# Slot places and norm rows moved between the gate and up products of a mixture-of-experts stage

## The chip, the core and the metric

The kernel runs on one core of a Trainium2 chip. The metric is the device time of one execution in microseconds (us): the median of several runs. The core has five engines that work side by side and wait for each other by semaphores: TensorE (PE; PEld is its weight load), VectorE (DVE), ScalarE (ACT), GpSimd (POOL) and SyncE (SP, which issues the DMAs here).

## What is computed

The reference is a decoder trunk of two layers over 512 tokens of width 1024, in float32. Each layer has a token mixer (attention in layer 0, a pooling mixer in layer 1), a layer norm, a mixture of 32 SwiGLU experts with two experts chosen per token, and another layer norm. The change touches the mixture alone:

```python
def run_block(args):
    xb, e = args
    h = jax.nn.silu(xb @ w_gate[e]) * (xb @ w_up[e])
    return h @ w_down[e]
...
out = jnp.zeros((N, D), x.dtype).at[tok_pad].add(y * w_pad[:, None].astype(y.dtype))
...
h = layer_norm(DEEPNORM_ALPHA * h + ffn, ln_g[i, 1], ln_b[i, 1])
```

Gate and up weights are 1024 x 512 per expert, down weights 512 x 1024: 6 MB per expert in float32, 384 MB for both layers.

## The kernel before

Function `moe` handles a layer's mixture. Experts are taken in 16 pairs; each expert of a pair has 64 slots (`CAP`), so a pair fills the 128 columns or rows of a tile. The loop over `q` (8 passes) handles two pairs, an even one `2q` and an odd one `2q + 1`. For a pair the work is:

- **Gather.** `G` is a matrix of zeros and ones that says which token sits in which slot, built for two pairs at once by VectorE (lines 583 and 584, eight instructions). TensorE multiplies the tokens with it (line 919) in four rounds of 16 products of 128 x 256 for each of two chunks; each round fills one PSUM bank, which ScalarE and VectorE empty into `xT`, scaled by the first norm's gain (lines 903, 905). In this kernel the rounds take the banks `ga`, `tp`, `ga`, `tp` in turn.
- **Gate and up.** `gate_up` makes 16 products for the gate (`psg`) and 16 for the up projection (`psu`), line 960, each two instructions in the trace, since a float32 product takes two; the two experts of a pair use the two halves of the array's columns. ScalarE makes silu of the gate (`sg`), VectorE multiplies (`h`, line 969).
- **Flip and down.** `flip` transposes `h` on TensorE into bank `tp` (line 974), ScalarE copies it to `hT`, and `down` makes 16 products `y` (line 985; 32 instructions). ScalarE and VectorE scale `y` by the slot's weight `ws` into `yy` as a high and a low part (lines 994, 995).
- **Places.** `places` transposes `G` of a pair into bank `ga` (line 934), which ScalarE copies to `Sm`; four products with the routing weights `wd` (`pw`, line 938) give, through `pwc`, the slot weights `ws`. Both pairs' places are made in the even pair's turn, just ahead of its down product.
- **Spread.** `spread_all` brings `yy` of the two pairs of the pass before back to the tokens through `Sm` (lines 1161, 1162, eight banks of four products, in the two `sc` banks); VectorE adds each bank to the residual `R` (line 1164). It stands in the even pair's turn, around the flip.

Two pieces occur once a layer. In pass 0, `whole` sums the tokens into `R` on GpSimd (line 1135), and after the odd pair's gather `residue` makes four norm rows (`norm_row`, line 384, four products or eight instructions each, with the gain or shift broadcast) which VectorE applies to `R` (lines 1143, 1145). In the last pass, `norm_rows` makes four rows of the second norm in bank `ga`, each copied by ScalarE into `gb` (line 390), between the spreads and the places.

`wd` of all pairs comes at the start of the stage out of a chain on VectorE and ScalarE that runs beside the first gate product (lines 1037 to 1048 and 257). GpSimd's `whole` runs beside it. After the last pair, where the routing needs it, `seek` and `down_spread` handle one extra item in the same way, and `norm_all` ends the layer.

TensorE's order in this stage is the order in which the code is written (`manual_schedule` for PE); the other engines' orders are made by a scheduler. Weight loads are issued by SyncE in one queue (`fill`, `take`), each into one of 21 buffers of 1 MB (`unit`) as soon as the work that read the buffer before is done.

Of the kernel before, what the change touches and what calls it, by code (L numbers as in the profile page):

```python
# [41 lines left out]
WARM2 = 2  # L42
REGION = {mybir.EngineType.PE, mybir.EngineType.DVE, mybir.EngineType.Activation, mybir.EngineType.Pool}
# [21 lines left out]
def tile_trunk(ctx, tc, x, w_qkv, w_o, p_in, p_grp, p_scale, p_out,  # L65
# [826 lines left out]
    def moe(l, rt_in, name1, after):  # L892
        with ExitStack() as es:
# [13 lines left out]
            def gather(slots, cc, xT, pairs):  # L907
# [16 lines left out]
                def ga_tile(k0):  # L924
                    return p1.tile([P, 2, 2 * P], F32, name="ga", tag=("ga", "tp")[k0 // 2 % 2])
# [3 lines left out]
            def places(G, i, wd, Sm, ws):  # L929

                ga = p1.tile([P, NT, P], F32, name="ga", tag="ga")
                gi = G[:, :, i * P:(i + 1) * P]
                for j, t in enumerate(tiles):
                    PE.transpose(ga[:, t], gi[:, j].bitcast(F32), ident)
                ACT.activation(Sm[:, :].rearrange("p (t q) -> p t q", t=NT), ga, AF.Copy)
                pw = p1.tile([P, 4], F32, name="pw", tag="tp")
                for t in range(NT):
                    PE.matmul(pw, gi[:, t], wd[:, t], start=t == 0, stop=t == NT - 1)
                pc = mo.tile([P, 4], F32, name="pwc", tag="pwc")
                V.tensor_copy(pc, pw)  # L940
                for e in range(2):
                    es_ = slice(e * CAP, (e + 1) * CAP)
                    V.tensor_tensor(ws[es_], pc[es_, e:e + 1], pc[es_, 2 + e:3 + e], op=OP.add)
# [138 lines left out]
            def place(G, p):  # L1082
                Sm = mo.tile([P, S], F32R, name="Sm", tag="Sm", bufs=3)
                ws = mo.tile([P, 1], F32, name="ws", tag="ws", bufs=3)
                places(G, p % 2, wd[:, :, p], Sm, ws)
                plc[p] = Sm, ws

            def seek(xT1, Sm1):
# [22 lines left out]
                places(G1, 0, wx, Sm1, ws1)  # L1111
# [15 lines left out]
            def bank():  # L1127
                return p1.tile([P, 512], F32, name="row", tag="ga")

# [7 lines left out]
            def residue(q, tag):  # L1137

                ps = norm_row(l, 0, q, p2.tile([P, 512], F32, name="row", tag=tag))
                for t in tiles:  # L1140
                    r = tok(R, t)[:, q % 2 * 512:(q % 2 + 1) * 512]
                    if q < 2:
                        V.scalar_tensor_tensor(r, r, ALPHA, ps, op0=OP.mult, op1=OP.mult)
                    else:
                        V.scalar_tensor_tensor(r, ps, ALPHA, r, op0=OP.mult, op1=OP.add)
# [6 lines left out]
            def spread_all(c, ys):  # L1152

                for t in range(NT):
                    spread_sum([(yr, Sm) for yr, Sm in ys], t, c)
# [10 lines left out]
            def gate_of(p):  # L1166
                h = h_tile()
                gate_up(xT[:, :, (p % 2) * P:(p % 2 + 1) * P],
                        [[take(nm, l, p, e) for e in range(2)] for nm in "gu"], h)
                done(8)  # L1170
                return h
# [10 lines left out]
            for q in range(NPAIR // 2):  # L1182
# [3 lines left out]
                h = gate_of(p)  # L1186
# [6 lines left out]
                if prev:  # L1193
                    spread_all(0, prev)
                hT = hT_tile()
# [3 lines left out]
                if final:  # L1199
                    gb, rows_ = norm_rows(l, 1, bank)  # L1200
                    do(rows_)
                place(G, p)
                place(G, p + 1)
# [4 lines left out]
                h = gate_of(p)  # L1208
# [19 lines left out]
                else:  # L1228
                    fill(CAPW)
                    xT, (G, rounds) = gather2(p + 1)  # L1230
                    rows_ = [lambda i=i: residue(i, "sc") for i in (0, 2, 1, 3)] if q == 0 else []
# [3 lines left out]
                    do(rounds[2:4] + rows_)  # L1235
# [110 lines left out]
```

## Time and profile before

| | |
|---|---|
| median of 3 runs | 1574.7 us (1573.53 to 1575.3) |
| the profiled execution | 1572.45 us |
| its span | 1570.7 us |
| TensorE busy | 1459.1 us (93%), 7477 instructions |
| VectorE busy | 629.3 us (40%) |
| ScalarE busy | 364.3 us (23%) |
| GpSimd busy | 102.0 us (6%) |
| read from HBM | 446.74 MB, 286 GB/s over the span |

The profile comes from one execution; the difference between its time and its span is 1.75 us. Mixture 0 runs from about 311 us, mixture 1 from about 1026 us of the span, each with eight passes. A row of a timeline gives the start, the duration up to the end of the last instruction of the row, the engine and line, what is written and read, how often, and in brackets the engine's idle time before it with what ended it. Rows that follow each other overlap by the latency of an instruction, so lengths are best taken from start to start. A row of windows gives a stretch and its length, then the busy time of PE, PEld, DVE, ACT and POOL with the number of instructions, TensorE's granted clock (1.00 is 2.4 GHz, 0.50 is 1.2 GHz; between them it is the mean over the stretch), the share of time that the DMA engines were busy, and their rate in GB/s. The stretches below begin and end where rows of TensorE's timeline begin: a repeating pass from odd gate product to odd gate product; the first pair of each layer from its up product to the next gate product; pass 0 from the end of the odd pair's up product to the next gate product; the last pass from its first norm row to the odd pair's gate product.

### The profile page before, as it was taken

What the parts mean: (1) busy time and instruction counts of PE and PEld (TensorE: products, weight loads), DVE (VectorE), ACT (ScalarE), POOL (GpSimd) and SP (SyncE); (2) the same over time, 40 slices, a digit from 0 to 9 for tenths busy, and PEclk for the clock granted to TensorE, in tenths of its full rate; (3) what the DMA queues carried; (4) which work ended last, traced back from release to release, by engine and by line L of the source; (5) the groups of instructions that cost most, each with busy time, mean ns of one, the idle gap of its engine ahead of it and who ended that gap; (6) DMA issues with size and microseconds to landing.
All of it is one profiled execution on the core that took longest, in us unless ns stands there. A gap on an engine that the chain in (4) does not pass through costs nothing. (4 is left out here: it accounts for less than half of the span.)

```text
span 1570.7 us, 18886 instructions
## 1 busy us (share of the span) xinstructions
PE 1459.1 (93%) x7477; PEld 838.0 (53%) x7477; DVE 629.3 (40%) x1447; ACT 364.3 (23%) x736; POOL 102.0 (6%) x66
## 2 busy tenths in 40 slices
PE   8999999998999999999998589998999999999993
PEld 6766777734544454445542467844455445444541
DVE  4366466643331322323233986653322213313216
ACT  4355464511111111111110323521111011111110
POOL 0000000320000000000004610230000000000001
PEclk9999999999999999999899899999999999999987
DMA  7111422677999999999865116567999999999921
GB/s 250 46 54 49 166 112 77 268 305 300 414 402 403 414 407 403 408 406 415 353 268 210 33 54 241 210 266 295 412 408 412 397 410 411 398 407 414 406 105 55
DMA packets 85571, 450.20 MB, mean 287 GB/s; under 512 B 10648, under 2 KB 20448, under 8 KB 36320
## 3 DMA queue, kind: packets, MB, share of 16 engines
q1 hardware_dynamic: 85472, 448.86, 71.6%
q8 instruction: 64, 1.05, 0.3%
q14 instruction: 35, 0.29, 0.1%
HBM read 446.74 MB, written 2.10 MB: 286 GB/s over the span
## 5 line engine op out<-in xcount | busy, mean ns | idle before, releaser
L960 PE MATMUL psg<-w_g,xT 128*64 128x512 f32 x1024 | 225.2, 592 | 0.2 <-ACT xT L903 0.2
L960 PE MATMUL psu<-w_u,xT 128*64 128x512 f32 x1024 | 225.1, 592 | 0.0
L985 PE MATMUL y<-w_d,hT 128*64 128x512 f32 x960 | 224.2, 622 | 0.0
L995 DVE SCALAR_TENSOR_TENSOR yy<-y,ws,yy 128x512 fp32r<-128x512 f32 x66 | 48.6, 737 | 395.1 <-ACT yy L994 394.4
L960 PEld LDWEIGHTS psu<-w_u,xT 128*64 128x64 f32 x1024 | 73.3, 137 | 146.4 <-issue 142.7
L960 PEld LDWEIGHTS psg<-w_g,xT 128*64 128x64 f32 x1024 | 73.1, 137 | 145.9 <-issue 141.4
L985 PEld LDWEIGHTS y<-w_d,hT 128*64 128x64 f32 x960 | 69.0, 143 | 131.1 <-issue 129.2
L919 PEld LDWEIGHTS ga<-G,xs 128*128 128x128 f32 x960 | 114.0, 188 | 12.2 <-issue 12.2
L919 PE MATMUL ga<-G,xs 128*128 128x256 f32 x960 | 119.6, 282 | 0.0
L967 ACT ACTIVATE sg<-psg 128x512 f32<-128x512 f32 x33 | 19.7, 597 | 423.5 <-PE psg L960 423.5
L1161 PE MATMUL sc<-yy,Sm 128*128 128x512 f32 x240 | 102.0, 425 | 6.7 <-DVE r L1164 6.1
L1164 DVE TENSOR_TENSOR r<-r,sc 128x512 f32<-128x512 f32 x128 | 85.9, 684 | 36.1 <-PE sc L1162 36.1
L969 DVE TENSOR_TENSOR h<-sg,psu 128x512 f32<-128x512 f32 x33 | 35.6, 1078 | 161.2 <-PE psu L960 150.4
L1162 PE MATMUL sc<-yy,Sm 128*128 128x512 f32 x240 | 94.8, 395 | 0.0
L288 PE MATMUL acc<-pc,xTh 128*128 128x512 f32 x192 | 77.6, 404 | 2.6 <-ACT pc L256 2.3
L289 PE MATMUL acc<-pc,xTh 128*128 128x512 f32 x192 | 77.1, 402 | 0.8 <-DVE pc L257 0.8
L290 PE MATMUL acc<-pc,xTl 128*128 128x512 f32 x192 | 77.6, 404 | 0.0
L905 DVE TENSOR_SCALAR xT<-ga,gcol 128x256 f32<-128x256 f32 (+1 forms) x60 | 32.1, 535 | 107.7 <-ACT xT L903 107.7
L903 ACT ACTIVATE xT<-ga,gcol 128x256 f32<-128x256 f32 (+1 forms) x60 | 33.4, 557 | 151.9 <-PE ga L919 151.9
L1161 PEld LDWEIGHTS sc<-yy,Sm 128*128 128x128 f32 x240 | 45.1, 188 | 41.9 <-DVE r L1164 22.1
L994 ACT ACTIVATE yy<-y,ws 128x512 fp32r<-128x512 f32 x66 | 45.2, 684 | 79.5 <-PE y L1013 36.2
L975 ACT ACTIVATE hT<-tp 128x512 f32<-128x512 f32 x33 | 19.7, 598 | 182.3 <-PE tp L974 182.3
(303 smaller groups left out, 1923.7 us busy)
## 6 DMA issues: line engine op xcount, KB each, us to landing
w_g<-in_moe_w_gate_dram SPq DMA_DIRECT2D x128, 1024.0 KB
w_u<-in_moe_w_up_dram SPq DMA_DIRECT2D x128, 1024.0 KB
w_d<-in_moe_w_down_dram SPq DMA_DIRECT2D x128, 1024.0 KB
w_a<-in_attn_w_qkv_dram SPq DMA_DIRECT2D x16, 512.0 KB
x<-in_x_dram SPq DMA_DIRECT2D x8, 512.0 KB
w_v<-in_attn_w_qkv_dram SPq DMA_DIRECT2D x4, 1024.0 KB
w_wo<-in_attn_w_o_dram SPq DMA_DIRECT2D x4, 1024.0 KB
wx<-in_moe_w_gate_dram SPq DMA_DIRECT2D x4, 1024.0 KB
```

Of the source, the lines that this page charges most:

```text
L288: PE.matmul(acc, xhl(0, k), wh, start=start and j == 0, stop=False)
L289: PE.matmul(acc, xhl(0, k), wl, start=False, stop=False)
L290: PE.matmul(acc, xhl(1, k), wh, start=False, stop=stop and j == len(order) - 1)
L919: PE.matmul(ga[:, k - k0], half_of(xs[j], i).bitcast(F32R)[:, k], g, start=j + i == 0, stop=j + i == NT)
L960: PE.matmul(ps[es_], xT[:, k, es_], ws2[e][k // 4][:, k % 4], start=k == 0, stop=k == KD - 1)
L969: V.tensor_tensor(h[:, :, :].rearrange("s k q -> s q k"), r(sg), r(gu[1]), op=OP.mult)
L985: PE.matmul(y[es_, c], hT[:, k, es_], wd(e, k, c), start=k == 0, stop=k == 3)
L994: ACT.activation(yr[:, c], y[:, c], AF.Copy, scale=wslot)
L995: V.scalar_tensor_tensor(yr[:, 2 + c], y[:, c], wslot, yy[:, c], op0=OP.mult, op1=OP.subtract)
L1161: PE.matmul(ps, sm, yr[:, c], start=i == 0, stop=False)
L1162: PE.matmul(ps, sm, yr[:, 2 + c], start=False, stop=i == len(ys) - 1)
L1164: V.tensor_tensor(r, r, ps, op=OP.add)
```

## The change

- `places` is cut into `flip_places` (the transposes of one pair into bank `ga` and the copy to `Sm`) and `slot_weights` (the eight `pw` products of two pairs, one copy, four additions). `place` hands out two lists. `gate_of` has a new argument `between`, and runs what is in it between the pair's last gate product and its first up product. The even pair gets its own transposes and both pairs' `pw` products there, the odd pair its own transposes.
- The norm rows go to the same gaps, two rows (eight products, 16 instructions) in a gap, in the `sc` banks: `residue` in the gaps of pairs 1 and 2, `norm_rows` in those of pairs 14 and 15.
- The gather's second and third rounds use the `sc` banks instead of `tp` and `ga`; the fourth uses `ga`.
- In pass 0, which has no spreads, 9 products of 128 x 256 in bfloat16 that nobody reads stand ahead of the transposes of `h`, and 5 behind them (`WARM5`, `WARM6`).

The arithmetic stays as it was. Blank lines are left out.

```diff
--- before.py
+++ after.py
@@ -40,6 +40,8 @@
 WARM3 = 24
 WARM4 = 10
 WARM2 = 2
+WARM5 = 9
+WARM6 = 5
 REGION = {mybir.EngineType.PE, mybir.EngineType.DVE, mybir.EngineType.Activation, mybir.EngineType.Pool}
 FILL2 = 3
@@ -922,25 +924,36 @@
                         factor(xT[:, k, 0:n], ga[:, k - k0, 0:n], k, (ACT, V)[k % 2])
                 def ga_tile(k0):
-                    return p1.tile([P, 2, 2 * P], F32, name="ga", tag=("ga", "tp")[k0 // 2 % 2])
+                    if k0 in (2, 4):
+                        return p2.tile([P, 2, 2 * P], F32, name="ga", tag="sc")
+                    return p1.tile([P, 2, 2 * P], F32, name="ga", tag="ga")
                 return G, [lambda k0=k0: round(k0, ga_tile(k0)) for k0 in range(0, KD, 2)]
-            def places(G, i, wd, Sm, ws):
-                ga = p1.tile([P, NT, P], F32, name="ga", tag="ga")
-                gi = G[:, :, i * P:(i + 1) * P]
+            def flip_places(G, i, Sm, ga):
                 for j, t in enumerate(tiles):
-                    PE.transpose(ga[:, t], gi[:, j].bitcast(F32), ident)
+                    PE.transpose(ga[:, t], G[:, j, i * P:(i + 1) * P].bitcast(F32), ident)
                 ACT.activation(Sm[:, :].rearrange("p (t q) -> p t q", t=NT), ga, AF.Copy)
-                pw = p1.tile([P, 4], F32, name="pw", tag="tp")
-                for t in range(NT):
-                    PE.matmul(pw, gi[:, t], wd[:, t], start=t == 0, stop=t == NT - 1)
-                pc = mo.tile([P, 4], F32, name="pwc", tag="pwc")
-                V.tensor_copy(pc, pw)
-                for e in range(2):
-                    es_ = slice(e * CAP, (e + 1) * CAP)
-                    V.tensor_tensor(ws[es_], pc[es_, e:e + 1], pc[es_, 2 + e:3 + e], op=OP.add)
+            def slot_weights(G, todo, pw):
+                for i, (wd, ws) in enumerate(todo):
+                    for t in range(NT):
+                        PE.matmul(pw[:, 4 * i:4 * i + 4], G[:, t, i * P:(i + 1) * P], wd[:, t],
+                                  start=t == 0, stop=t == NT - 1)
+                n = len(todo)
+                pc = mo.tile([P, 8], F32, name="pwc", tag="pwc")
+                V.tensor_copy(pc[:, 0:4 * n], pw[:, 0:4 * n])
+                for i, (wd, ws) in enumerate(todo):
+                    for e in range(2):
+                        es_ = slice(e * CAP, (e + 1) * CAP)
+                        V.tensor_tensor(ws[es_], pc[es_, 4 * i + e:4 * i + e + 1],
+                                        pc[es_, 4 * i + 2 + e:4 * i + 3 + e], op=OP.add)
+            def places(G, wd, Sm, ws):
+                flip_places(G, 0, Sm, p1.tile([P, NT, P], F32, name="ga", tag="ga"))
+                slot_weights(G, [(wd, ws)], p1.tile([P, 8], F32, name="pw", tag="tp"))
             def run(todo):
                 if todo:
@@ -1080,10 +1093,15 @@
             plc = {}
             def place(G, p):
-                Sm = mo.tile([P, S], F32R, name="Sm", tag="Sm", bufs=3)
-                ws = mo.tile([P, 1], F32, name="ws", tag="ws", bufs=3)
-                places(G, p % 2, wd[:, :, p], Sm, ws)
-                plc[p] = Sm, ws
+                for i in range(2):
+                    Sm = mo.tile([P, S], F32R, name="Sm", tag="Sm", bufs=3)
+                    ws = mo.tile([P, 1], F32, name="ws", tag="ws", bufs=4)
+                    plc[p + i] = Sm, ws
+                flips = [lambda i=i: flip_places(G, i, plc[p + i][0], p1.tile([P, NT, P], F32, name="ga", tag="ga"))
+                         for i in range(2)]
+                return [flips[0], lambda: slot_weights(G, [(wd[:, :, p + i], plc[p + i][1]) for i in range(2)],
+                                                       p1.tile([P, 8], F32, name="pw", tag="tp"))], flips[1:]
             def seek(xT1, Sm1):
@@ -1108,7 +1126,7 @@
                 V.tensor_scalar(rem, rem, 0.0, None, op0=OP.max)
                 G1, rounds = gather(sl, code, xT1, 1)
                 do(rounds)
-                places(G1, 0, wx, Sm1, ws1)
+                places(G1, wx, Sm1, ws1)
             def fetch(w, pr, u2):
                 wv = w[l].rearrange("e (p k) n -> e p (k n)", p=P)
@@ -1124,9 +1142,6 @@
                         nc.sync.dma_start(u2[c][e], wv[bass.ds(pr[e], 1), :, :, c * 512:(c + 1) * 512]
                                           .rearrange("a p k n -> (a p) k n"))
-            def bank():
-                return p1.tile([P, 512], F32, name="row", tag="ga")
             def whole(c):
                 for j, t in enumerate(tiles):
@@ -1134,9 +1149,9 @@
                     hi, lo = [half_of(xs[j], i)[:, :, c * 64:(c + 1) * 64] for i in range(2)]
                     nc.gpsimd.tensor_tensor(rq, hi, lo, op=OP.add)
-            def residue(q, tag):
-                ps = norm_row(l, 0, q, p2.tile([P, 512], F32, name="row", tag=tag))
+            def residue(q):
+                ps = norm_row(l, 0, q, p2.tile([P, 512], F32, name="row", tag="sc"))
                 for t in tiles:
                     r = tok(R, t)[:, q % 2 * 512:(q % 2 + 1) * 512]
                     if q < 2:
@@ -1163,10 +1178,12 @@
                 r = tok(R, t)[:, c * 512:(c + 1) * 512]
                 V.tensor_tensor(r, r, ps, op=OP.add)
-            def gate_of(p):
+            def gate_of(p, between=()):
                 h = h_tile()
                 gate_up(xT[:, :, (p % 2) * P:(p % 2 + 1) * P],
-                        [[take(nm, l, p, e) for e in range(2)] for nm in "gu"], h)
+                        [[take(nm, l, p, e) for e in range(2)] for nm in "gu"], h,
+                        todo=[lambda: do(between)], at=(KD - 1,))
                 done(8)
                 return h
@@ -1183,7 +1200,13 @@
                 p, final = 2 * q, q == NPAIR // 2 - 1
                 fill(CAPW)
-                h = gate_of(p)
+                if final:
+                    gb, rows_ = norm_rows(l, 1, lambda: p2.tile([P, 512], F32, name="row", tag="sc"))
+                else:
+                    rows_ = [lambda i=i: residue(i) for i in (0, 2, 1, 3)]
+                placed, placed2 = place(G, p)
+                h = gate_of(p, placed if q == 0 else (placed + rows_[0:2] if final else
+                                                      placed + rows_[2:4] if q == 1 else placed))
                 if q == 0:
                     R = two("r")
                     whole(0)
@@ -1192,20 +1215,20 @@
                 fill(CAPW)
                 if prev:
                     spread_all(0, prev)
+                else:
+                    wps = p2.tile([P, 512], F32, name="wps", tag="sc")
+                    warm(wps, WARM5)
                 hT = hT_tile()
                 flip(h, hT)
                 if prev:
                     spread_all(1, prev)
-                if final:
-                    gb, rows_ = norm_rows(l, 1, bank)
-                    do(rows_)
-                place(G, p)
-                place(G, p + 1)
+                else:
+                    warm(wps, WARM6)
                 prev = [down_of(p, hT, wdn)]
                 p += 1
                 fill(5 if final else CAPW)
-                h = gate_of(p)
+                h = gate_of(p, placed2 + (rows_[2:4] if final else rows_[0:2] if q == 0 else []))
                 wdn = [take("d", l, p, i) for i in range(2)]
                 Sm, ws = plc[p]
                 if final:
@@ -1228,11 +1251,10 @@
                 else:
                     fill(CAPW)
                     xT, (G, rounds) = gather2(p + 1)
-                    rows_ = [lambda i=i: residue(i, "sc") for i in (0, 2, 1, 3)] if q == 0 else []
                     do(rounds[0:2])
                     hT = hT_tile()
                     flip(h, hT)
-                    do(rounds[2:4] + rows_)
+                    do(rounds[2:4])
                     prev.append(down_of(p, hT, wdn))
```

TensorE, even pair of pass 1 (`sc` is a spread, `ga` the transposes of `G`, `pw` the weight products, `row` norm rows, `y` a down product). Before, at the end of the spreads:

```order
L1162 MATMUL sc<-yy,Sm 128x512
L934 MATMUL ga<-cf,G 128x128 x4
L938 MATMUL pw<-wd,G 128x4 x4
L934 MATMUL ga<-cf,G 128x128 x4
L938 MATMUL pw<-wd,G 128x4 x4
L985 MATMUL y<-w_d_2_0_0_3224,hT 64x512
```

Now, between the pair's gate and up products (line numbers are the changed kernel's):

```order
L973 MATMUL psg<-w_g_2_1_1_3244,xT 64x512
L936 MATMUL ga<-cf,G 128x128 x4
L943 MATMUL pw<-wd,G 128x4 x8
L386 MATMUL row<-vec,cf 128x128 x8
L973 MATMUL psu<-w_u_2_0_0_3246,xT 64x512
```

The places left the stretch between spread and down product for the one between gate and up; in pass 1 two norm rows follow them.

TensorE, odd pair of pass 0, from the up product to the down product. Before:

```order
L960 MATMUL psu<-w_u_1_0_1_3095,xT 64x512
L960 MATMUL psu<-w_u_1_1_1_3097,xT 64x512
L919 MATMUL ga<-G,xs 128x256 x32
L974 MATMUL tp<-cf,h 128x128 x4
L919 MATMUL ga<-G,xs 128x256 x32
L384 MATMUL row<-vec,cf 128x128 x16
L985 MATMUL y<-w_d_1_0_0_3099,hT 64x512
```

Now, ahead of the up product:

```order
L973 MATMUL psg<-w_g_1_0_1_3036,xT 64x512
L973 MATMUL psg<-w_g_1_1_1_3038,xT 64x512
L936 MATMUL ga<-cf,G 128x128 x4
L386 MATMUL row<-vec,cf 128x128 x8
L973 MATMUL psu<-w_u_1_0_0_3040,xT 64x512
```

The 16 products of the norm rows no longer stand between the gather and the down product; eight of them follow the transposes of `G` here, the other eight stand in the next pair, above.

VectorE, odd pair of pass 0 (`G` is rebuilt for the next pass, `r` are the residue's steps). Before:

```order
L583 TENSOR_SCALAR G<-cf,cc 128x256
L943 TENSOR_TENSOR ws<-pwc 64x1 x2
L584 SCALAR_TENSOR_TENSOR G<-cf,cc,G 128x256
L583 TENSOR_SCALAR G<-cf,cc 128x256 x2
L584 SCALAR_TENSOR_TENSOR G<-cf,cc,G 128x256 x2
L583 TENSOR_SCALAR G<-cf,cc 128x256
L584 SCALAR_TENSOR_TENSOR G<-cf,cc,G 128x256
L1024 TENSOR_SCALAR cc<-code 128x8
L995 SCALAR_TENSOR_TENSOR yy<-y,ws,yy 128x512
L969 TENSOR_TENSOR h<-sg,psu 128x128x4
```

Now, between the first pair's `h` and the second's:

```order
L585 TENSOR_SCALAR G<-cf,cc 128x256 x2
L586 SCALAR_TENSOR_TENSOR G<-cf,cc,G 128x256 x2
L1158 SCALAR_TENSOR_TENSOR r_3109<-r_3109,row 128x512 x2
L1158 SCALAR_TENSOR_TENSOR r_3108<-r_3108,row 128x512 x2
L1160 SCALAR_TENSOR_TENSOR r_3109<-row,r_3109 128x512 x2
L1160 SCALAR_TENSOR_TENSOR r_3108<-row,r_3108 128x512 x2
L585 TENSOR_SCALAR G<-cf,cc 128x256 x2
L586 SCALAR_TENSOR_TENSOR G<-cf,cc,G 128x256
L1008 SCALAR_TENSOR_TENSOR yy<-y,ws,yy 128x512
L586 SCALAR_TENSOR_TENSOR G<-cf,cc,G 128x256
L1037 TENSOR_SCALAR cc<-code 128x8
L982 TENSOR_TENSOR h<-sg,psu 128x128x4
```

The residue's first eight steps stand inside the rebuilding of `G`, which now waits for the odd pair's transposes.

## Rows read from the trace of the kernel before

**Rows 1.** Windows: stretch, its us, busy us of the engines, clock, DMA share, GB/s

```profile
411.00:472.97 61.97, 60.09 (x315) 29.60 (x312) 16.21 (x33) 8.37 (x14) 0.00 (x0) 1.00 1.00 407
318.22:339.10 20.88, 18.09 (x87) 7.58 (x85) 12.61 (x33) 3.89 (x6) 7.32 (x6) 0.92 0.73 283
1033.01:1054.98 21.97, 19.59 (x87) 8.36 (x84) 12.23 (x32) 3.89 (x6) 7.29 (x6) 0.84 0.70 270
352.93:379.35 26.42, 21.99 (x136) 15.30 (x135) 13.39 (x22) 2.86 (x5) 0.00 (x0) 0.87 0.64 256
1068.81:1095.68 26.87, 22.43 (x134) 15.42 (x134) 13.40 (x22) 2.86 (x5) 0.00 (x0) 0.87 0.63 248
773.67:795.37 21.70, 18.91 (x82) 11.60 (x82) 1.63 (x7) 3.58 (x6) 0.00 (x0) 0.69 0.42 157
1490.13:1511.95 21.82, 19.03 (x81) 11.56 (x81) 1.63 (x7) 3.58 (x6) 0.00 (x0) 0.69 0.42 159
```

**Rows 2.** Waits of TensorE, 400 to 760 us: us in total, times, longest

```profile
PE tp L974 <- DVE xT L905: 7.4, 6, 1.2
```

**Rows 3.** Timeline of TensorE in a repeating pass: start us, us, instruction, [idle before]

```profile
401.86 0.60 PE L934 MATMUL ga<-cf,G 128*128 128x128 f32 x4
...
403.15 0.66 PE L934 MATMUL ga<-cf,G 128*128 128x128 f32 x4 [0.34 <-ACT Sm L935]
403.56 0.59 PE L938 MATMUL pw<-wd,G 128*128 128x4 f32 x4
404.08 7.09 PE L985 MATMUL y<-w_d,hT 128*64 128x512 f32 x32
411.00 7.04 PE L960 MATMUL psg<-w_g,xT 128*64 128x512 f32 x32
417.86 7.04 PE L960 MATMUL psu<-w_u,xT 128*64 128x512 f32 x32
424.83 4.00 PE L919 MATMUL ga<-G,xs 128*128 128x256 f32 x32
430.07 0.66 PE L974 MATMUL tp<-cf,h 128*128 128x128 f32 x4 [1.24 <-DVE xT L905]
...
434.39 7.09 PE L985 MATMUL y<-w_d,hT 128*64 128x512 f32 x32
```

**Rows 4.** Timeline of TensorE: unread products, norm rows, the extra item's pair

```profile
304.63 0.60 PE L307 MATMUL acc<-cb 128*128 128x256 bf16 x4
...
362.40 1.95 PE L384 MATMUL row<-vec,cf 72*128 72x128 f32 x16
...
847.53 7.04 PE L960 MATMUL psu<-wx,xT 128*64 128x512 f32 x32
855.89 0.63 PE L974 MATMUL tp<-cf,h 128*128 128x128 f32 x4 [1.33 <-DVE h L969]
857.27 3.72 PE L1013 MATMUL y<-wx,hT 128*64 128x512 f32 x16 [0.75 <-ACT hT L975]
```

**Rows 5.** Timeline of VectorE: the last step of wd, the residue steps

```profile
320.84 0.90 DVE L257 TENSOR_TENSOR wd<-wsum,wd 128x128 fp32r<-128x128 f32 x1 [0.40 <-ACT wd L256]
...
363.65 2.47 DVE L1143 SCALAR_TENSOR_TENSOR r<-r,row 128x512 f32<-128x512 f32 x4
...
1034.36 0.90 DVE L257 TENSOR_TENSOR wd<-wsum,wd 128x128 fp32r<-128x128 f32 x1 [0.39 <-ACT wd L256]
```

**Rows 6.** Groups of instructions on VectorE, whole run: x count | busy us, mean ns

```profile
L995 DVE SCALAR_TENSOR_TENSOR yy<-y,ws,yy 128x512 fp32r<-128x512 f32 x66 | 48.6, 737 | 395.1 <-ACT yy L994 394.4 <-ACTq L1254 0.4 <-ACTq L1246 0.3
...
L584 DVE SCALAR_TENSOR_TENSOR G<-cf,cc,G 128x256 fp32r<-128x256 f32 x56 | 25.8, 481 | 0.9
...
L583 DVE TENSOR_SCALAR G<-cf,cc 128x256 fp32r<-128x256 f32 x56 | 18.4, 349 | 0.4
```

**Rows 7.** Timeline of SyncE in a repeating pass

```profile
424.92 16.91 SPq L147 DMA_DIRECT2D w_d<-in_moe_w_down_dram  x4
```

**Rows 8.** DMA rate in 40 equal slices of 411 to 597 us

```profile
GB/s 423 425 421 423 423 421 305 403 423 428 423 423 361 370 402 430 426 423 418 403 361 428 430 423 418 421 338 428 428 418 423 421 375 342 419 425 423 423 423 324
```

## Prediction

> **What bounds the kernel now.** I looked first at the stretches of the mixture stages. Between the two gate products of one repeating pass (two pairs of experts) lie 61.97 us, of which TensorE is busy 60.09 at clock 1.00 [rows 1]; it bounds that stage. The list of TensorE's waits in 400 to 760 us has three lines, none of them a DMA; the first is 1.24 us, once a pass, where the transposes of h wait for VectorE to empty the `tp` bank [rows 2, 3]. In the ordered timeline of one pass everything else stands back to back but the places, where the second set of transposes waits 0.34 us for ScalarE [rows 3]. The two ends of the stage look otherwise: from the end of the last up product of pass 0 to the next gate product 26.42 and 26.87 us (layers 0 and 1), and in pass 7 from the first norm row to the next gate product 21.70 and 21.82 us, at clocks 0.87 and 0.69 [rows 1]. Both have norm rows in series with vector work, and half-clock time behind them. TensorE's rows follow the program's order, so what is saved on it here moves everything after it.
>
> **The repeating passes (1 to 6, both layers: 12).** The gather's second and third rounds get the `sc` banks, which only spreads use and which VectorE emptied in the even pair's turn; `tp` is then free when the transposes of h come. h itself is no obstacle: after an up product the wait for it is 1.33 us [rows 4], and two rounds of products lie between. So the 1.24 us go: 12 × 1.24 = **-14.9**. Nothing new is late: round 3 takes `ga`, last filled by round 0, more than 4 us earlier.
>
> The places took 404.08 - 401.86 = 2.22 us a pass [rows 3]. They keep every instruction. One set of four transposes takes 403.56 - 403.15 = 0.41, four weight products 404.08 - 403.56 = 0.52 [rows 3], so eight take 1.04. Going from the half-array products to full ones costs 0.11 (an up product and its end take 424.83 - 417.86 = 6.97 against 6.86 for the gate) [rows 3]. Hence 0.41 + 1.04 + 0.11 = 1.56 in the gap of the even pair and 0.52 in that of the odd pair, 2.08 against 2.22. The waits of the old order have cover now: the copies on ScalarE and VectorE run beside 7 us of up products. That is 12 × 0.14 = **-1.7**. No trace row shows a switch back from full to half products by itself; I take 0, with 0.3 (about the 0.34 wait) a gap as the upper bound, 32 gaps, +10, and none below.
>
> **Pass 0 and the norm rows.** The new stretch is two rounds, transposes, two rounds (434.39 - 424.83 - 1.24 = 8.32) and a down product (411.00 - 404.08 = 6.92) [rows 3], 15.24 us against 26.42 and 26.87: -11.2 and -11.6. The norm rows go into two gaps, two rows each: eight products of the code, 16 instructions of the trace (float32 takes two); 16 took 1.95 us where banks were free [rows 4]. With the odd pair's transposes: 0.52 + 2 × 1.95 = +4.4 a layer. Sum of both layers: **-14.0**. Their two banks are emptied by VectorE beside the up product. In pass 0 G can only be rebuilt after the odd pair's transposes, so VectorE must do in that window eight G steps at 0.349 and 0.481 (3.3 us), eight residue steps (four took 2.47 [rows 5]) and one yy step at 0.737 [rows 6]: about 9.0 us. TensorE gets to the first product that needs the last quarter of G after 1.95 + 6.97 + six of the 32 products of two rounds (0.7), 9.6 us. I count 0; bound, were GpSimd or the order to slow VectorE, 1.5 a layer.
>
> **Pass 7.** 21.70 and 21.82 shrink to a down product, 6.92, plus gaps of 2.08 and 2 × 1.95: 12.9. That is -8.8 and -8.9, **-17.7**. The half clock in the old stretch is in these numbers. The copies of the rows on ScalarE leave the path, since nothing on TensorE follows them but the spreads, 7 us later.
>
> **The first pair.** Here the change adds a wait. The weight products need `wd`, whose last step on VectorE ends at 320.84 + 0.90 = 321.74 in layer 0 and 1034.36 + 0.90 = 1035.26 in layer 1 [rows 5]; the gate product ends at 318.22 and 1033.01 [rows 1]. Behind the waiting product stand the whole up product, h and the down product. So in layer 0: products 321.8 to 322.9, up product, and transposes of h 855.89 - 847.53 = 8.36 later, down product 857.27 - 855.89 = 1.38 after that [rows 4], at 332.6, with 6.92 ending at 339.5 against 339.10: +0.4. In layer 1: 1035.3, 1036.4, 1044.7, 1046.1, 1053.0 against 1054.98: -2.0, since the old down product ran partly at half clock (0.84 over the stretch [rows 1]). The 9 and 5 unread products stand in waits of 1.33 and 0.75 [rows 4]; four like them take 0.60 with their latency [rows 4], so nine at most 1.35 and five at most 0.75: hidden. At half clock they would last twice that, up to 1.3 and 0.8 us late. Together **-1.6**.
>
> The weight loads keep their order; one buffer (for the norm's rows) is taken a load earlier. SyncE waits for buffers, not the reverse: the four issues of a down weight stretch over 16.91 us [rows 7].
>
> **Sum:** -14.9 - 1.7 - 14.0 - 17.7 - 1.6 = -49.9 us. The profiled execution took 1572.45, so 1522.5; the median of the runs, 1574.7, lies 2.25 higher, and gives 1524.8.
>
> **Rivals.**
>
> *The weight stream becomes the bound.* For it: the DMA share is 1.00 at 407 GB/s [rows 1], and a pass needs 24 loads of 1024 KB, 25.2 MB, so 61.8 us at 407; then the passes gain 0.2 instead of 1.4 each, 12 × 1.2 = 14.4 us less, 1539. Against it: in most slices of three passes the rate is 418 to 430, with dips to 305 and 338 [rows 8] where the queue had run dry behind a late buffer. At 423 a pass needs 59.5 us, under the 60.6 forecast. The Trainium skill (HBM Reference, Specifications) gives a core that streams alone about 425 GB/s; by that figure my estimate is 59.2 us a pass, and the full gain stands; by the 407 of the row it would not. Chance 0.07.
>
> *The clock falls at the first pair.* The new wait (3.1 us in layer 0, 1.9 in layer 1) and the thin weight products stand together; the old first pair, with a wait and thin products, shows clocks 0.92 and 0.84 [rows 1], that is 2 × 0.08 × 20.88 = 3.3 and 2 × 0.16 × 21.97 = 7.0 us at half speed, half of it lost. The same again costs up to 1.7 and 3.5 us: 1526 to 1530. Chance 0.23.
>
> *VectorE late at the gather of pass 0, or dearer gaps.* 3 to 13 us less gain, 1528 to 1538. Chance 0.12.
>
> *Slower: the clock falls in the gaps of every pass.* Gate and up products now have transposes, 4-column products and norm rows between them. In the old pass 7 such products, with waits, ran in a stretch at clock 0.69 over 21.70 us [rows 1]: 13.5 us at half speed, 6.7 lost. Once in each of 16 passes this is 107 us: 1632. It decides from 3.1 us a pass, where all 50 are gone. Against it: 2.2 us of the same transposes and weight products, with a wait inside, stood in every pass that shows clock 1.00 [rows 1, 3], and each new gap is shorter and between dense products. The Trainium skill (TensorE: Matmul & The Clock Gate, Part 4) says that transposes don't count as activity for the clock in the way products do, which speaks for this rival; the row at 1.00 speaks against it here. Chance 0.03.
>
> *The change doesn't do it.* The built order shows the products in the gaps, so only a bank that is still held could undo it; I saw none. No difference: 0.02.
>
> **How the numbers follow.** Forecast as summed: 0.53, its own range 1520 to 1529; then 0.23, 0.12, 0.07, 0.03, 0.02 as above. The range 1517 to 1537 takes in the clock's case and most of the dearer gaps. A measurement can tell about 0.2%, 3.1 us. Faster than that: 0.95; no difference 0.02; slower 0.03.
>
> **What would show it.** Right: no line in which the transposes of h wait for xT; a pass of 60.5 us between even gate products at clock 1.00; the 26 to 27 us from the end of pass 0's last up product to the next gate product shrunk to 15 to 16 us; the pass 7 stretch from spread to gate product about 7 us; no half clock there. Wrong: a DMA among TensorE's waits in the passes (stream), half clock within passes (slower), an up product that waits on more than `wd`, or the first pair ending later than 341 in layer 0.

## The result, and the profile after

The changed kernel takes 1533.87 us in the median of four runs (1531.86 to 1535.13), beside 1574.12 for the kernel before in runs on the same chip: a ratio of 0.9744, interval 0.9727 to 0.9761, or 40.3 us less. The forecast was 49.9 us less and 1524.8. The profiled execution took 1535.13 us with a span of 1533.3, so the two profiles show 37.4 of those 40.3 us (1570.7 - 1533.3).

The stretches of [rows 1] in the changed kernel stand in this order: a repeating pass; the first pair of each layer, from the end of its gate product (where the places now stand ahead of the up product) to the next gate product; pass 0; pass 7 from the last spread to the next gate product, now without norm rows and places in it. Columns as in [rows 1].

```profile
405.81:466.46 60.65, 60.34 (x314) 29.27 (x312) 15.87 (x32) 8.11 (x14) 0.00 (x0) 1.00 1.00 414
318.77:341.44 22.67, 19.58 (x96) 8.00 (x96) 9.12 (x23) 3.28 (x5) 7.19 (x6) 0.92 0.71 262
1019.64:1041.08 21.44, 19.62 (x96) 7.96 (x96) 8.73 (x22) 3.28 (x5) 7.14 (x6) 0.92 0.75 277
357.80:372.83 15.03, 15.03 (x102) 10.33 (x102) 3.84 (x6) 2.79 (x5) 0.00 (x0) 1.00 0.95 380
1057.44:1072.47 15.03, 15.03 (x102) 10.33 (x102) 3.84 (x6) 2.79 (x5) 0.00 (x0) 1.00 0.94 372
764.71:771.63 6.92, 6.92 (x33) 2.35 (x34) 0.69 (x1) 0.00 (x0) 0.00 (x0) 1.00 0.90 317
1464.38:1471.30 6.92, 6.92 (x34) 2.35 (x35) 0.69 (x1) 0.00 (x0) 0.00 (x0) 1.00 0.87 303
```

The ends of the stages did what the sum said: 26.42 and 26.87 us became 15.03 twice, 21.70 and 21.82 became 6.92 plus gaps, all at clock 1.00. The first pairs did not: 22.67 us against 20.88 in layer 0, where +0.4 was summed, and 21.44 against 21.97 in layer 1, where -2.0 was summed. The next fence is TensorE's timeline of the changed kernel: that first pair, a pass's two gaps, and pair 15 with the extra item behind it.

```profile
318.77 0.66 PE L936 MATMUL ga<-cf,G 128*128 128x128 f32 x4
322.22 1.10 PE L943 MATMUL pw<-wd,G 128*128 128x4 f32 x8 [2.79 <-DVE wd L259]
323.25 8.69 PE L973 MATMUL psu<-w_u,xT 128*64 128x512 f32 x32
...
341.44 7.04 PE L973 MATMUL psg<-w_g,xT 128*64 128x512 f32 x32
...
405.81 7.04 PE L973 MATMUL psg<-w_g,xT 128*64 128x512 f32 x32
...
412.77 0.66 PE L936 MATMUL ga<-cf,G 128*128 128x128 f32 x4
413.36 7.09 PE L973 MATMUL psu<-w_u,xT 128*64 128x512 f32 x32
...
435.40 7.04 PE L973 MATMUL psg<-w_g,xT 128*64 128x512 f32 x32
442.37 0.66 PE L936 MATMUL ga<-cf,G 128*128 128x128 f32 x4
442.78 1.03 PE L943 MATMUL pw<-wd,G 128*128 128x4 f32 x8
443.74 7.09 PE L973 MATMUL psu<-w_u,xT 128*64 128x512 f32 x32
...
780.97 7.09 PE L973 MATMUL psu<-w_u,xT 128*64 128x512 f32 x32
792.23 10.17 PE L921 MATMUL ga<-G,xs 128*128 128x256 f32 x64 [4.17 <-DVE G L586]
803.39 0.66 PE L936 MATMUL ga<-cf,G 128*128 128x128 f32 x4 [0.99 <-DVE xT L907]
```

In layer 0's first pair the up product takes 8.69 us, where others take 7.09, behind the wait for `wd`. At 788.06 the last up product ends, and the gather of the extra item waits 4.17 us for its G. No line of the diff moves the steps that build this G. The gather then takes 10.17 us (7.74 without the wait, in a run below) at a granted clock of 0.74, so part of it runs at half clock. The cause stands in VectorE's timeline of the changed kernel:

```profile
782.29 0.75 DVE L1008 SCALAR_TENSOR_TENSOR yy<-y,ws,yy 128x512 fp32r<-128x512 f32 x1 [1.04 <-ACT yy L1007]
788.13 1.03 DVE L982 TENSOR_TENSOR h<-sg,psu 128x512 f32<-128x512 f32 x1 [5.10 <-PE psu L973]
789.17 0.39 DVE L1110 TENSOR_SCALAR hit<-cf,ixf 128x32 f32<-128x32 f32 x2
...
792.73 0.61 DVE L586 SCALAR_TENSOR_TENSOR G<-sl,code,G 128x128 fp32r<-128x128 f32 x2
```

and, of the kernel before, the same steps in the other order:

```profile
797.84 0.75 DVE L995 SCALAR_TENSOR_TENSOR yy<-y,ws,yy 128x512 fp32r<-128x512 f32 x1 [0.76 <-ACT yy L994]
798.87 0.39 DVE L1092 TENSOR_SCALAR hit<-cf,ixf 128x32 f32<-128x32 f32 x2 [0.28 <-DVE yy L995]
...
803.76 0.61 DVE L584 SCALAR_TENSOR_TENSOR G<-sl,code,G 128x128 fp32r<-128x128 f32 x2
...
819.13 1.04 DVE L969 TENSOR_TENSOR h<-sg,psu 128x512 f32<-128x512 f32 x1
```

VectorE's order is left to the scheduler here; only TensorE's is written by hand. Before, the item's steps ran beside the last up product (802.23 to 809.20) and `h` of pair 15 came after them. Now `h` stands ahead and waits 5.10 us for that up product, and the item's steps stand behind it.

Where the time went, from the start of one gate (or up) product to the next in both profiles, beside the forecast for the same stretch:

| stretch | forecast | measured |
|---|---|---|
| first pairs, gate 0 to gate 1 | +0.4, -2.0 | 27.79 to 29.69, 28.89 to 28.46: +1.5 |
| pass 0, gate 1 to gate 2 | -17.9 | 40.25 and 40.70 to 31.39 twice: -18.2 |
| passes 1 to 6, gate 2 to gate 14 (with two norm rows) | -12.7 | 371.79 to 365.86, 371.92 to 365.88: -12.0 |
| pass 7, gate 14 to up 15 | -17.7 | 51.09 to 42.28, 51.22 to 42.29: -17.7 |
| up 15 of layer 0 to gate 0 of layer 1 | 0 | 223.86 to 231.65: +7.8 |
| before gate 0 of layer 0, and behind up 15 of layer 1 | 0 | +0.4, +0.8 |

### The profile page after: what moved, and what is told of

It reads as the page before. It is cut to its first block, busy times and chain, and to the rows that moved or that the text cites. A ratio compares the mean times of both kernels' runs of the same rounds, so it can differ in the third digit from the quotient of the medians.

```text
span 1533.3 us, 18931 instructions
## 1 busy us (share of the span) xinstructions
PE 1451.5 (95%) x7505; PEld 827.7 (54%) x7505; DVE 623.6 (41%) x1431; ACT 359.7 (23%) x736; POOL 101.8 (7%) x66
## 5 line engine op out<-in xcount | busy, mean ns | idle before, releaser
L973 PE MATMUL psu<-w_u,xT 128*64 128x512 f32 x1024 | 230.1, 602 | 0.0
L998 PE MATMUL y<-w_d,hT 128*64 128x512 f32 x960 | 212.6, 595 | 0.3
L585 DVE TENSOR_SCALAR G<-cf,cc 128x256 fp32r<-128x256 f32 x56 | 17.2, 350 | 197.4 <-PE ga L936 197.4
```

Of the source, the lines that this page charges most:

```text
L973: PE.matmul(ps[es_], xT[:, k, es_], ws2[e][k // 4][:, k % 4], start=k == 0, stop=k == KD - 1)
L998: PE.matmul(y[es_, c], hT[:, k, es_], wd(e, k, c), start=k == 0, stop=k == 3)
```

## Experiments

The runs were made in three sessions, and a difference between two kernels is that of their medians. The kernel before, run in each session, had medians of 1572.83 to 1573.46 us there and 1574.12 beside the changed kernel, so about 1 us of a difference across sessions can be the session.

**The extra item.** VectorE in written order from the item on, with `h` written behind it; the sums that the gather doesn't need stand behind G:

```diff
...
-                    with tc.If(n_items, preferred_fallthrough_block=False):
+                    with tc.manual_schedule(engines={mybir.EngineType.PE, mybir.EngineType.DVE}):
+                        with tc.If(n_items, preferred_fallthrough_block=False):
...
+                        do(held)
```

> The changed kernel, with VectorE kept in written order around the extra item and the product h of pair 15 written behind the item's steps; the sums for wx and rem stand behind the item's G steps. TensorE's order is the same. Theory (VectorE's order makes the item late): G is ready at the end of pair 15's up product, the 4.17 us wait of the item's first gather product is gone or under 0.6 us, the gather stands at full clock (7.7 us instead of 10.2) and the flip behind it no longer waits 0.4 us longer; together 7 to 8 us less than the changed kernel's 1533.9, so 1526 to 1527. Rival (the clock falls there whether TensorE waits or not): only the wait goes, 4.2 us less, 1529.7. Rival (G is held by pair 15's transposes): nothing changes, 1534.

Measured: 1527.13 us (ratio to before 0.972, 0.9706 to 0.9733), 6.7 less than the changed kernel and a little under the 7 to 8 that were expected. TensorE's timeline of this kernel:

```profile
780.09 7.09 PE L973 MATMUL psu<-w_u,xT 128*64 128x512 f32 x32
787.11 7.74 PE L921 MATMUL ga<-G,xs 128*128 128x256 f32 x64
795.84 0.66 PE L936 MATMUL ga<-cf,G 128*128 128x128 f32 x4 [0.99 <-DVE xT L907]
```

The gather follows the up product at once, at clock 1.00: the wait of 4.17 us and the 2.43 us of half clock behind it (10.17 - 7.74) are gone together. From the start of the up product to the transposes behind the gather it is 15.75 us instead of 22.42, which is the 6.7. The rival cause was G's buffer, which pair 15's transposes now read later than before:

```diff
-                h = gate_of(p, placed if q == 0 else (placed + rows_[0:2] if final else
+                h = gate_of(p, placed if q == 0 else (placed + placed2 + rows_[0:2] if final else
...
-                h = gate_of(p, placed2 + (rows_[2:4] if final else rows_[0:2] if q == 0 else []))
+                h = gate_of(p, rows_[2:4] if final else placed2 + (rows_[0:2] if q == 0 else []))
```

Only pass 7's transposes move; what the expectation says of all odd pairs doesn't hold for this kernel.

> The changed kernel, with pair 15's transposes of places moved into pair 14's gap, as all odd transposes into the even pair's gap, so that nothing reads G any more when pair 15 begins. VectorE's order is unchanged. Theory (VectorE's order makes the item late): the 4.17 us wait for G stays, and so does the time, 1533 to 1536 (pass 0's G may be rebuilt sooner, which gives nothing, since no wait stands there; the even gap has two sets of transposes in one bank, which may cost 0.3 us in each of 16 passes, up to 5 us). Rival (the item's G is held by pair 15's transposes, which the change put later): the wait goes, 1526 to 1530.

Measured: 1533.85 us (0.9756, 0.9741 to 0.9771). The wait, in TensorE's timeline of this kernel, is unchanged:

```profile
792.24 9.10 PE L921 MATMUL ga<-G,xs 128*128 128x256 f32 x64 [4.17 <-DVE G L586]
```

So VectorE's order made the item late, and not the transposes. The half clock behind the same wait took 1.36 us in this execution (9.10 - 7.74) instead of 2.43, so its size isn't fixed. What in the change made the scheduler turn the two around stays open. The gather's new banks, which the item's gather uses too, did not: in e_rounds below, which has that edit alone, the item's gather starts at 797.41 us, as the up product ends, without a wait.

**The first pair.** The slot weights behind the up product, in the `ga` bank, and 2 unread products instead of 9:

```diff
...
-                h = gate_of(p, placed if q == 0 else (placed + rows_[0:2] if final else
+                h = gate_of(p, placed[0:1] if q == 0 else (placed + rows_[0:2] if final else
...
+                    placed[1]()
                     warm(wps, WARM5)
```

> The changed kernel, with pair 0's and pair 1's slot weights computed behind pair 0's up product instead of ahead of it (in the bank that the first transposes used), and 2 unread products instead of 9 beside them. Theory (the wait for wd brings the half clock into the first up product): the up product starts 0.1 us after the first transposes, without the waits of 2.79 and 1.52 us, and takes 6.97 instead of 8.69 and 8.78 us; the 1.04 us of slot weights hide in the wait for h; 4.0 + 1.7 in layer 0 at most, 2.5 + 1.8 in layer 1, less what of the half clock returns later: 6 to 10 us less than 1533.9, so 1524 to 1528. Rival (the clock falls at the first pair whatever stands there, as it did before the change): only the waits go, 2.8 + 1.5 and about 1 us for the products, 1528.5 to 1530.

Measured: 1524.56 us (0.9701, 0.9687 to 0.9715), 9.3 less than the changed kernel. Windows of this kernel, from the end of the first gate product to the next gate product, in layers 0 and 1, columns as in [rows 1]:

```profile
317.62:335.29 17.67, 17.03 (x89) 6.88 (x89) 9.21 (x23) 3.29 (x5) 7.21 (x6) 1.00 0.92 333
1011.92:1029.57 17.65, 17.04 (x90) 6.87 (x90) 8.94 (x22) 3.29 (x5) 7.20 (x6) 1.00 0.92 336
```

22.67 and 21.44 us at clock 0.92 became 17.67 and 17.65 at 1.00, 8.8 us in both. More goes than the waits (2.79 and 1.52) and the products (2.1): the half clock goes with them.

**Both edits together.**

> The two edits together: VectorE's order at the extra item, and the slot weights of the first two pairs behind the up product. If the two losses are apart from each other and both theories hold, the gains add: 1533.9 - 7.5 - 8 = 1518, between 1516 and 1522. If the clock only falls elsewhere, less than 9 us is gained: 1525 or more.

Measured: 1518.76 us (0.9658, 0.9645 to 0.967), 15.1 less than the changed kernel against 6.7 + 9.3 = 16.0: the two losses are apart from each other within about 1 us. The first is most of what the forecast missed; the second gives back more than was missed there, since the wait for `wd` had been counted.

**The gather's banks alone**, put into the kernel before:

```diff
-                    return p1.tile([P, 2, 2 * P], F32, name="ga", tag=("ga", "tp")[k0 // 2 % 2])
+                    if k0 in (2, 4):
+                        return p2.tile([P, 2, 2 * P], F32, name="ga", tag="sc")
+                    return p1.tile([P, 2, 2 * P], F32, name="ga", tag="ga")
```

> The kernel before, with one edit of the change alone: the gather's second and third rounds take the sc banks. Theory (each pass's 1.24 us wait of the transposes of h is the whole of it and nothing takes its place): 12 to 14 times 1.24 us less, 14.9 to 17.4, from 1573.5 to 1574.1: 1556 to 1559; the two passes in which the norm rows follow the rounds may give nothing, since the rows then wait for the same banks. Rival (VectorE's xT steps or h come next): less than 8 us, 1566 or more.

Measured: 1551.55 us (0.9864, 0.9849 to 0.9879), 21.3 less than before in the same session, and more than theory or rival expected. Passes 1 to 6 give 17.1 of it in the profiles (gate 2 to gate 14 363.25 and 363.36 us, against 371.79 and 371.92); the rest lies at the ends of the stages and has no cause shown. This kernel's pass in a window, and the rows of TensorE's timeline between its two rounds:

```profile
409.01:469.55 60.54, 59.88 (x315) 29.63 (x312) 16.22 (x33) 8.30 (x14) 0.00 (x0) 1.00 1.01 415
```

```profile
422.85 4.01 PE L919 MATMUL ga<-G,xs 128*128 128x256 f32 x32
426.69 0.60 PE L976 MATMUL tp<-cf,h 128*128 128x128 f32 x4
427.05 3.98 PE L919 MATMUL ga<-G,xs 128*128 128x256 f32 x32
430.96 7.09 PE L987 MATMUL y<-w_d,hT 128*64 128x512 f32 x32
```

From the first round to the down product 8.11 us against 9.56 [rows 3], 1.45 less for a wait of 1.24. The rest is on both sides of the wait: the two rounds take 3.84 us to the start of the transposes (422.85 to 426.69) instead of 4.00 to the start of the wait, and from the transposes to the down product it is 4.27 instead of 4.32. The pass takes 60.54 us. With the whole change it takes 60.65, so the places in the gaps cost each pass 0.1 instead of saving 0.14.

**The norm rows back in series** in the kernel of e_both (in each of both ends, four rows in the place where they were):

```diff
-                                                      placed + rows_[2:4] if q == 1 else placed))
+                                                      placed))
...
-                    do(rounds[2:4])
+                    do(rounds[2:4] + (rows_ if q == 0 else []))
```

> The kernel of e_both (1518.8 us) with the norm rows put back where they stood before the change: pass 0's four behind the gather's rounds, pass 7's four behind the spreads; everything else stays. Theory (the ends of the stage were dear because of the rows' waits and the half clock behind them): in each layer pass 0's rows take 8.3 us in series instead of 3.9 in the gaps, pass 7's 9.1 instead of 3.9, 9.6 us a layer and 19 in both; half clock behind them costs 2 to 5 us at each of the four places, so 27 to 39 us in all: 1546 to 1558. Rival (it was the places in series that brought the half clock, not the rows): only the 19 us, 1538.

Measured: 1531.43 us (0.974, 0.9726 to 0.9753), 12.7 more than e_both, less than theory and rival. Pass 0 costs 5.9 and 6.1 us more (gate 1 to gate 2 39.18 and 39.34, against 31.40 and 31.39 in e_both, less 1.9 in the gap of pass 1), pass 7 only 0.1. The last two norm rows of pass 0 and all four of pass 7, each with the down product behind them, in TensorE's timeline of this kernel:

```profile
362.07 1.64 PE L386 MATMUL row<-vec,cf 72*128 72x128 f32 x8 [1.93 <-DVE r L1161]
364.47 2.05 PE L386 MATMUL row<-vec,cf 72*128 72x128 f32 x8 [0.76 <-DVE r L1163]
366.44 8.51 PE L1002 MATMUL y<-w_d,hT 128*64 128x512 f32 x32
...
762.80 3.93 PE L386 MATMUL row<-vec,cf 72*128 72x128 f32 x32
766.66 7.09 PE L1002 MATMUL y<-w_d,hT 128*64 128x512 f32 x32
```

In pass 0 the rows wait for VectorE's steps, and the down product behind them takes 8.51 us instead of 7.09. In pass 7, where ScalarE empties the two `sc` banks, four rows take 3.86 us without a wait, about as long as in the gaps. So the same kernel with pass 7's rows in the one `ga` bank:

```diff
-                    gb, rows_ = norm_rows(l, 1, lambda: p2.tile([P, 512], F32, name="row", tag="sc"))
+                    gb, rows_ = norm_rows(l, 1, lambda: p1.tile([P, 512], F32, name="row", tag="ga"))
```

> The kernel of e_rowsold (1531.4 us: the norm rows in series, pass 7's in the two sc banks), with pass 7's rows in the single ga bank, as before the change. It shows what the bank is worth there. Theory (the waits of 0.69 us for ScalarE's copy bring the half clock with them): four waits of 0.69 us and 2 to 5 us of lost clock in each layer, 9 to 15 us more: 1541 to 1546. Rival (the half clock in pass 7 came from the places that stood behind the rows): only the waits, 5.5 us more, 1537.

Measured: 1539.95 us (0.9797, 0.9777 to 0.9817), 8.5 more than e_rowsold, between theory and rival. Its rows, and its window over them and the down product beside that of e_rowsold:

```profile
761.85 1.05 PE L386 MATMUL row<-vec,cf 72*128 72x128 f32 x8
763.59 1.16 PE L386 MATMUL row<-vec,cf 72*128 72x128 f32 x8 [0.69 <-ACT gb L392]
...
767.28 1.86 PE L386 MATMUL row<-vec,cf 72*128 72x128 f32 x8 [0.69 <-ACT gb L392]
769.07 8.00 PE L1002 MATMUL y<-w_d,hT 128*64 128x512 f32 x32
```

```profile
761.85:776.90 15.05, 12.99 (x65) 6.92 (x65) 0.69 (x1) 2.39 (x4) 0.00 (x0) 0.89 0.51 186
```

```profile
762.80:773.58 10.78, 10.78 (x65) 6.09 (x66) 0.69 (x1) 2.39 (x4) 0.00 (x0) 1.00 0.73 269
```

15.05 against 10.78 us, 4.27 in each layer: three waits of 0.69 and a clock of 0.89, that is 2 × 0.11 × 15.05 = 3.3 us at half speed, 1.7 lost. Of the 8.9 us a layer that pass 7 gave, the second bank is 4.3. The place between gate and up products is at most 0.1 of it. The rest I put down to the places, which stood behind these rows, after a fourth wait and at half clock, in the kernel before (3.49 us to the down product, against 2.15 in the gaps):

```profile
782.78 1.11 PE L934 MATMUL ga<-cf,G 128*128 128x128 f32 x4 [0.69 <-ACT gb L390]
...
786.27 9.26 PE L985 MATMUL y<-w_d,hT 128*64 128x512 f32 x32
```

That part was not run alone.

**The unread products**, left out of the changed kernel and of e_both's (which has 2 instead of 9):

```diff
-WARM5 = 9
-WARM6 = 5
+WARM5 = 0
+WARM6 = 0
```

> The changed kernel (1533.9 us) without the 9 and 5 unread products at the first pair of each layer. Theory (they only fill waits for h and hT, at no price and no gain): within 1.5 us of 1533.9. Rival (they hold the clock up): half clock then reaches into the first down product or the next gate product, 1.7 to 3.4 us a layer, 1537 to 1541.

> The kernel of e_both (1518.8 us) without unread products (2 and 5 there), the slot weights still behind the up product. The same two theories where no half clock stands in the first pair: no effect, 1518 to 1520; or the clock falls behind the waits for h and hT, 1.7 to 3.4 us a layer, 1522 to 1526.

> The kernel of e_both_nowarm a second time. Theory (the unread products buy nothing): equal to e_both_2 within 1.5 us, and whether the half clock stands in layer 0's first down product, as in its first profile, changes from run to run. Rival (they hold the clock in layer 0): the half clock stands there again, 1.6 us in the first pair, and the time is 1 to 2 us above e_both_2.

Measured: 1534.48 us against 1533.87; 1517.60 (0.9654, 0.9641 to 0.9667) against 1518.76; in the second run 1519.74 (0.9667, 0.9649 to 0.9685) against e_both_2's 1518.76. The sign changes, all are within 1.2 us. Half clock stood in layer 0's first pair in one profile of e_both's kernel without them (26.30 us from gate to gate), not in the other (24.68); with them it is 24.68 and 24.69. They buy nothing that these runs can tell.

**The places in series in the passes.** The kernel of e_both again, and the same with the places of passes 1 to 6 behind the spreads, in the order transposes, all eight weight products, transposes (in the gaps of these passes the places are left out; that part of the edit is not shown):

```diff
...
+                    if not final:
+                        do(placed + placed2)
```

> The kernel of e_both a second time, beside the next three on one chip: 1518.8 within 2 us; no half clock in the first pair of either layer, as in its first profile.

> The kernel of e_both, with the places of passes 1 to 6 back in series behind the spreads, in the order transposes, both pairs' slot weights, transposes, so that no set of transposes waits for ScalarE; passes 0 and 7 keep them in the gaps. Theory (a gap between half products costs about 0.1 us each time TensorE goes from half products to full ones and back, so the places in gaps cost the steady passes more than in series): a pass of 60.2 to 60.4 us instead of 60.66, 12 times 0.3 to 0.44, 3.5 to 5.3 us less: 1513.5 to 1515.5. Rival (the copies on ScalarE and VectorE want the cover of the up product): a wait of 0.3 us or more takes the saving back, 1518 to 1522.

Measured: 1518.76 us for e_both_2 (0.9655, 0.9638 to 0.9673), 1512.37 for e_mixed (0.962, 0.96 to 0.9639), the fastest kernel of this study: 6.4 us under e_both, 21.5 under the changed kernel. The passes give 5.4 of the 6.4 in the two profiles (gate 2 to gate 14 363.18 and 363.22, against 365.88 twice), a little more than the expected 3.5 to 5.3; the last 1 us lies outside them and has no cause shown. Its pass:

```profile
427.87:488.07 60.20, 59.89 (x315) 29.50 (x313) 15.99 (x32) 8.30 (x14) 0.00 (x0) 1.00 1.01 417
```

```profile
427.87 7.04 PE L973 MATMUL psg<-w_g,xT 128*64 128x512 f32 x32
434.74 7.04 PE L973 MATMUL psu<-w_u,xT 128*64 128x512 f32 x32
...
450.41 0.60 PE L936 MATMUL ga<-cf,G 128*128 128x128 f32 x4
450.76 1.03 PE L943 MATMUL pw<-wd,G 128*128 128x4 f32 x8
451.69 0.66 PE L936 MATMUL ga<-cf,G 128*128 128x128 f32 x4
452.28 7.09 PE L1002 MATMUL y<-w_d,hT 128*64 128x512 f32 x32
```

In series the places take 452.28 - 450.41 = 1.87 us, with no wait, since the weight products stand between the two sets of transposes. In the changed kernel's gaps they take 8.34 - 6.87 = 1.47 (435.40 to 443.74, against 427.87 to 434.74 here) and 7.55 - 6.87 = 0.68 (405.81 to 413.36). That is 2.15, and more than this series or the old one without its wait (2.22 - 0.34 = 1.88). A gate product takes 0.10 longer from start to start when transposes follow it (6.97, 435.40 to 442.37), and the odd gap's four transposes take 0.59 to the up product (412.77 to 413.36) where four take 0.41 to a full product [rows 3]: going out of the half products and back costs 0.28 in the odd gap. Around the gaps, too, a little is lost. An up product behind places takes 7.02 from start to start (443.74 to 450.76), 6.96 here (434.74 to 441.70), and the second half of the spreads takes 4.01 to the down product (455.53 to 459.54), 3.93 to the places here (446.48 to 450.41). With 2.15 - 1.87 = 0.28 for the places, 2 × 0.06 and 0.08 make the 0.48 us by which the passes differ (60.66 and 60.18 in most of them). The Trainium skill (TensorEngine Tiling (Array Packing), Key Properties) says that a change of tiling mode drains TensorE; these rows agree, at 0.10 us on the way out and 0.18 on the way back; no run separates such a drain from other causes.

## Why the prediction was right in sign and 10 us too hopeful

- **Passes, gather wait:** right in mechanism (no transposes of h wait for xT any more), sized low: 1.43 us a pass in e_rounds (61.97 to 60.54) for 1.24. That the passes together came near the sum, 12.0 for 12.7, is in part luck: this error and the next, of the opposite sign, nearly cancel.
- **Places:** wrong in sign: 0.1 dearer in the gaps, not 0.14 cheaper. The step that failed is the way back from full to half products, taken as 0 (with 0.3 a gap as the bound; the way out was counted, at 0.11). It took 0.18 in the odd gap, the two gaps 2.15 where 2.08 was summed, and the up products and the spreads around them 0.18 a pass more than in e_rounds. The copies on ScalarE, whose cover was to pay, needed only another order (e_mixed).
- **Pass 0:** right. Gate 1 to gate 2 fell by 18.2 for 17.9, TensorE did not wait for G, and with the norm rows back in series 5.9 and 6.1 us return (e_rowsold).
- **Pass 7:** right in size (17.7 for 17.7), with a wrong reason for the norm rows: the second bank ended their waits, and their place gave nothing.
- **The first pair:** +1.5 for -1.6. The wait for `wd` came as summed (2.79 us, products from 322.2); the rival of the clock came true behind it. The pairs ended 1.5 and 1.6 us over the sum, where the rival was priced at up to 1.7 and 3.5. A sign of being wrong that the prediction names came too: the first pair of layer 0 was to end no later than 341 and ended at 341.44, though 0.4 of that stood ahead of its gate product.
- **What the sum left out:** "what is saved on it here moves everything after it". That step failed. The sum ended at pair 15's up product, and took the extra item behind it as it was. The change had also moved VectorE's steps there, which cost 6.7 us (e_seek). This is most of the 10 us. So the measured time lies in the stated range, 1517 to 1537, partly by luck: the range was widened for the clock at the first pair and for dearer gaps, and most of the 9.1 us over the forecast came from a wait that no rival named. The rival "VectorE late" looked at the gather of pass 0, where no wait came.
- **The weight stream** did not bind. The pass runs at 414 GB/s without a DMA among its waits, and in e_mixed at 417 with 60.20 us. The figure of about 425 GB/s in the Trainium skill (HBM Reference, Specifications) is not contradicted.
- **Half clock in every gap** did not happen: the passes show 1.00 with transposes in the gaps. The Trainium skill's remark on transposes (TensorE: Matmul & The Clock Gate, Part 4) spoke for it; in these gaps the measurement decides against it.

## What to carry to other kernels

When a scheduler orders an engine, compare that engine's order at every place where another waits for it, also where the edit has nothing: here a product of the next step moved ahead of an index chain and cost 6.7 us. A thin product that waited cost its wait and the clock behind it here; put such a product where its operand is ready. Give a series that waits for its bank to be emptied a second bank before moving it. Work in a gap isn't free, and a copy can also be covered by a change of order in the series.

## What was not expected of the hardware

A wait of 1.24 us was worth 1.45 when it went, since the products on both sides of it also moved closer, by 0.16 and 0.05. The same transposes and weight products took 2.15 us in two gaps between half-array products and 1.87 in one series behind full ones. Three waits of 0.69 us between norm rows came with half clock in the rows and the down product behind them (clock 0.89 over the stretch); the same rows without a wait showed 1.00.
